# Tokens on ScalarE's queue, and the first quarter of a projection in halves, in a two-layer trunk step

## The chip, the cores and the metric

The kernel runs on one core of a Trainium2 chip. The metric is the device time of one execution in microseconds (us). A core has five engines that run in order, each with its own instruction stream: PE (matrix products), DVE (vector), ACT (ScalarE, activations and copies), POOL (GpSimd) and SP (which mostly issues transfers). Transfers between the chip's memory and the on-core memory are issued by SP or ACT on a hardware queue of each, or by POOL on a software queue, and are carried by 16 DMA engines. A transfer's landing is told by a semaphore; whatever needs it waits for that semaphore.

## What is computed

One inference step of a two-layer trunk for 512 sample tokens and 128 prompt tokens (640 together, width 2048, float32). Cut to what matters here:

```python
sh_p, sc_p, gt_p = modulation(c_ctx, ada_w[layer], ada_b[layer])   # silu(cond) @ w + b, in three parts of 2048
sh_s, sc_s, gt_s = modulation(c, ada_w[layer], ada_b[layer])
hp = rms_norm(xp, norm_g[layer]) * (1.0 + sc_p) + sh_p
hs = rms_norm(xs, norm_g[layer]) * (1.0 + sc_s) + sh_s
...                                                                # mixer: (h @ w_in) -> attention, convolution, gates
xp = xp + gt_p * out_p                                             # out = y @ w_out
xs = xs + gt_s * out_s
```

The first input projection needs h, and h needs the tokens' norms, the scale sc and the shift sh of the first layer. The conditioning matrix `ada_w` is 2048 x 6144 for each layer; it is cut into 12 blocks of 512 columns (4 MB each). Blocks 0 to 3 are the shift, 4 to 7 the scale, 8 to 11 the gate. The change touches the loads and the conditioning ahead of and inside the first input projection.

## The kernel before, in words

*Start.* Small vectors (the two conditions, norms, biases) are loaded into rows (`rows_a`, `rows_b`, L92 to L102), one on SP's queue and ten on ACT's. ACT takes a tanh of the conditions (L109), PE transposes the rows (L113, L114). Then `x_load` issues the tokens on SP's queue: five blocks of 128 tokens, each in two loads of 128 x 1024 (512 KB), into buffers that later hold h. `x_block` transposes a block with PE into PSUM in four groups (L839), copies the groups out (three on DVE, one on ACT, L840), squares and sums on ACT (L844), and has POOL take the power -0.5 (L848). `x_rows` (L854, L855) spreads the norms over a table of rows.

*Conditioning.* `ada_on_pe(l, cb, h, n)` computes n x 128 columns of block cb: it loads 2 MB at a time into one of two buffers (`ada_t`, L154), multiplies with the conditions (L157, 128x512 or, for a half block, 128x256), copies (L160), transposes (L163), reduces and adds the bias on DVE (L165, L145, L134). A whole block is two loads, half a block one. Blocks 4 and 0 give scale and shift for the first quarter of the width; before the change both are computed whole ahead of the projection.

*The projection.* `run_tiles` takes the 2048-wide sum in four quarters of four 128-row pieces each. For six leading tiles it goes quarter by quarter, so that only the part of h that is ready is needed: for each quarter (a unit) it loads the weights (`load_raw`, L233, 256 KB a tile in a whole unit), splits each into a rounded part and a remainder (`split_w`: ACT L220, DVE L221), makes h (`h0_maker`: DVE L878, ACT L882, DVE L883), and multiplies three times per piece and half of the tokens (L255, L256, L257): 144 products for a whole unit of six tiles. Four of the six tiles (`trans`) add the units up in memory: ACT copies the first unit's sums (L319), DVE adds the later ones (L321). Ahead of the second tile of a unit, `ahead` (`ada_group`) computes the two conditioning blocks for the next unit. The last quarter is cut into two halves (`cut`), which have half blocks and loads of 128 KB. The last call of `ada_group` also loads gains, the band and the sink (L71, L863).

*What sets the order.* The program is written in source order, but a scheduler places each engine's instructions and the transfers of each queue by its own costs; the built order of a queue can differ from the source's. Weight buffers (`raw`) are four; the rows at the start use three of them. Transfers from SP and ACT share eight semaphores in turn, so that a transfer also waits until the one that had its semaphore before has landed.

Of the kernel before, what the change touches and what calls it, by code (L numbers as in the profile page):

```python
# [11 lines left out]
F32 = mybir.dt.float32  # L12
# [8 lines left out]
P = 128  # L21
# [20 lines left out]
W_BUFS = 4  # L42
# [11 lines left out]
def trunk_kernel(ctx: ExitStack, tc: tile.TileContext, I: dict, O: dict):  # L54
    nc = tc.nc
# [3 lines left out]
    hpool = ctx.enter_context(tc.tile_pool(name="h", bufs=1))  # L59
# [7 lines left out]
    def psT():  # L67
        return pT.tile([P, 512], F32, tag="T", name="T")
# [14 lines left out]
    ident = const.tile([P, P], F32, name="ident")  # L83
# [5 lines left out]
    open_pool("start")  # L89
    sp = pre = pools["cur"]  # L90
    rows_a = wpool.tile([P, P], F32, tag="raw", name="rows_a")
    nc.sync.dma_start(rows_a[0:16, :], I["c"].rearrange("b (k p) -> (b k) p", p=P))  # L92
    nc.scalar.dma_start(rows_a[16:32, :], I["c_ctx"].rearrange("(k p) -> k p", p=P))
    nc.scalar.dma_start(ident, I["k_ident"])
    nc.scalar.dma_start(rows_a[32:64, :], I["norm_g"].rearrange("l (k p) -> (l k) p", p=P))
    nc.scalar.dma_start(rows_a[64:112, :], I["ada_b"][0].rearrange("(k p) -> k p", p=P))
    rows_b = wpool.tile([P, P], F32, tag="raw", name="rows_b")
    nc.scalar.dma_start(rows_b[0:48, :], I["ada_b"][1].rearrange("(k p) -> k p", p=P))
    nc.scalar.dma_start(rows_b[48:72, :], I["b_conv"][0].rearrange("t (k p) -> (t k) p", p=P))
    nc.scalar.dma_start(rows_b[72:74, :], I["c_out_norm"].rearrange("b (k p) -> (b k) p", p=P))  # L100
    for i, n in enumerate(("a_q_norm", "c_q_norm", "d_q_norm")):
        nc.scalar.dma_start(rows_b[74 + i:75 + i, :], I[n])  # L102
# [15 lines left out]
    norm_g = [vec[:, 0:16], vec[:, 16:32]]  # L118
    ada_b = [vec[:, 32:80], vec[:, 80:128]]
# [23 lines left out]
    def add_bias(l, cb, red, h=0, n=4):  # L143
        fs = slice(cb * 4 + 2 * h, cb * 4 + 2 * h + n)
        V.tensor_tensor(mod[l][:, fs, :], red, ada_b[l][:, fs][:, :, None].to_broadcast([P, n, 2]), op=ALU.add)  # L145

    def ada_on_pe(l, cb, h=0, n=4):

        acc, m, wd = psT(), 32 // n, n * P
        for kt in range(KT):  # L150
            if kt % m == 0:
                w = ada_t[0].rearrange("p (k n) -> p k n", k=m)
                ada_t.reverse()
                nc.sync.dma_start(w, I["ada_w"][l, kt * P:(kt + m) * P, cb * 512 + h * 256:cb * 512 + h * 256 + wd]  # L154
                                  .rearrange("(k p) n -> p k n", p=P))
            g = kt % 4
            PE.matmul(acc[32 * g:32 * g + 32, 0:wd], sT[:, kt, :], w[:, kt % m, :],  # L157
                      start=(kt < 4), stop=(kt >= KT - 4), tile_position=(0, 32 * g))
        sb = ada_sb
        A.copy(sb[:, 0:wd], acc[:, 0:wd])  # L160
        tr = psT()
        for j in range(n):
            PE.transpose(tr[:, j * P:(j + 1) * P], sb[:, j * P:(j + 1) * P], ident)  # L163
# [67 lines left out]
    def load_raw(w_ap, col, qd, js=(0, 4)):  # L231
        raw = wpool.tile([P, js[1] - js[0], P], F32, tag="raw", name="raw")
        nc.sync.dma_start(raw, w_ap[(qd * 4 + js[0]) * P:(qd * 4 + js[1]) * P, col:col + P]  # L233
                          .rearrange("(k p) n -> p k n", p=P))
        return raw
# [3 lines left out]
    def split_w(raw):  # L239
        wh = wpool.tile(raw.shape, F32R, tag="wh", name="wh")  # L240
        wl = wpool.tile(raw.shape, F32R, tag="wl", name="wl")
        split(wh, wl, raw)
        mark[0] = wl[:, 0, 0:1]
        return wh, wl
# [41 lines left out]
            credit[0] -= 1.0  # L286

    def run_tiles(jobs, w_ap, make_h, fill=None, rate=0.0, ahead=None, order=(0, 1, 2, 3), before=None,
                  last=None, by_half=False, trans=[], grace=0, cut=None, summed=None, led=None, fill_from=0):
        if trans:  # L290
            lp = tc.tile_pool(name="lead", bufs=1, side="right")
            lead_pool = lp.__enter__()
# [3 lines left out]
            leads = [n for m in range(len(held) + 1) for n in trans[m:m + 1] + held[m:m + 1]]  # L296
            leads += trans[len(held) + 1:]
        else:
            leads, held, lp = list(range(min(3, len(jobs)))), [], None
        lead = len(leads)  # L300
        pps = {n: (sums[n][:, 0:HALF], sums[n][:, HALF:NT]) if n in trans
               else new_pp(1 + held.index(n) if trans else n) for n in leads}
        units = [(pos, qd, js) for pos, qd in enumerate(order) for js in (cut if cut and pos == 3 else [(0, 4)])]
        for ui, (pos, qd, js) in enumerate(units):
            parts = {n: split_w(load_raw(w_ap, jobs[n][0], qd, js)) for n in leads[:W_BUFS]}
            for hv in [HV[:1], HV[1:]] if by_half and pos == 0 else [HV]:
                for k in range(4 * qd + js[0], 4 * qd + js[1]):
                    make_h(k, hv) if by_half else make_h(k)
                for n in leads:
                    if ahead and n == leads[1] and ui + 1 < len(units):  # L310
                        ahead(*units[ui + 1][1:])
                    if n not in parts:
                        parts[n] = split_w(load_raw(w_ap, jobs[n][0], qd, js))
                    if n in trans:
                        pp = new_pp(0)
                        proj_q(pp, parts[n], qd, pos, alone=True, js=js)
                        for i, sl in HV:
                            if ui == 0:
                                A.copy(pps[n][i], pp[i][:, 0:HALF])  # L319
                            else:  # L320
                                V.tensor_add(pps[n][i], pps[n][i], pp[i][:, 0:HALF])  # L321
# [9 lines left out]
        raws, parts = {}, {}  # L331
# [36 lines left out]
        t = 0  # L368
        if before:
            settle()  # L370
        else:
            n = pending.pop(0)
            begin(jobs[n][1], pps[n])
        for i in range(lead, len(jobs)):
# [3 lines left out]
            for qd in range(4):  # L378
# [5 lines left out]
                if pending and not prep:  # L384
                    n = pending.pop(0)
# [436 lines left out]

    rows = tables[:, 0:NT]

    def x_load(b):
        src = I["x_sample"][0, b * P:(b + 1) * P, :] if b < 4 else I["x_prompt"][0]
        ts = []
        for g in range(2):
            ts.append(hpool.tile([P, 1024], F32, tag=f"h{15 - 2 * b - g}", name="xb"))
            nc.sync.dma_start(ts[g], src[:, g * 1024:(g + 1) * 1024])  # L830
        return ts

    def x_block(b, ts):
        s4 = small.tile([P, 2], F32, tag="s4", name="s4")
        for g in range(4):
            ta = psT()
            for j in range(4):
                o = g % 2 * 512 + j * P
                PE.transpose(ta[:, j * P:(j + 1) * P], ts[g // 2][:, o:o + P], ident)  # L839
            (A.copy if g == 3 else V.tensor_copy)(xT[g][:, :, b * P:(b + 1) * P],  # L840
                                                  ta.rearrange("p (j t) -> p j t", j=4))
            if g % 2 == 0:
                junk = pS.tile([P, 1024], F32, tag="S", name="sqj")
                A.activation(junk, ts[g // 2], AF.Square, accum_out=s4[:, g // 2:g // 2 + 1])  # L844
# [12 lines left out]
    def ada_group(g, js):  # L857
        for cb in (4 + g, g):
            ada_on_pe(0, cb, js[0] // 2, js[1] - js[0])
        if g == 3 and js[1] == 4:  # L860
# [2 lines left out]
            nc.sync.dma_start(band, I["k_band"])  # L863
# [129 lines left out]
    jobs = []  # L993
# [5 lines left out]
    for i in range(4):  # L999
        kv, h = i // 2, 2 * i  # L1000
# [8 lines left out]
    for i in range(4, 8):  # L1009
# [349 lines left out]
    jobs = []  # L1359
# [14 lines left out]
    for n in range(4):  # L1374
        kv, h = n // 2, 2 * n
# [109 lines left out]
```

## Time and profile before

| | us |
|---|---|
| median of three runs | 2332.34 (2330.66 to 2336.76) |
| the profiled execution, device time | 2336.12 |
| its span, first to last instruction | 2334.1 |
| PE busy | 2288.0 (98%) |
| DVE busy | 1566.7 (67%) |
| ACT busy | 928.8 (40%) |

Mean granted clock of PE is 0.995. Times in rows are microseconds from the span's start unless marked ns; a row of the timeline gives start, duration, engine, line, operation, output<-input and the count of merged instructions, and in brackets how long the engine had stood idle before and what it waited for. "SPq" and "ACTq" are the transfer issues of these engines. PEld is PE's weight load, which overlaps PE. A busy PE includes matmuls that overlap each other in its pipeline. The stretch that the change touches is the first 160 us, up to the end of the six leading tiles.

### The profile page before, as it was taken

What the parts mean: (1) busy time and instruction counts of PE and PEld (TensorE: products, weight loads), DVE (VectorE), ACT (ScalarE), POOL (GpSimd) and SP (SyncE); (2) the same over time, 40 slices, a digit from 0 to 9 for tenths busy, and PEclk for the clock granted to TensorE, in tenths of its full rate; (3) what the DMA queues carried; (4) which work ended last, traced back from release to release, by engine and by line L of the source; (5) the groups of instructions that cost most, each with busy time, mean ns of one, the idle gap of its engine ahead of it and who ended that gap; (6) DMA issues with size and microseconds to landing.
All of it is one profiled execution on the core that took longest, in us unless ns stands there. A gap on an engine that the chain in (4) does not pass through costs nothing.

```text
span 2334.1 us, 41243 instructions
## 1 busy us (share of the span) xinstructions
PE 2288.0 (98%) x15924; PEld 2207.8 (95%) x15924; DVE 1566.7 (67%) x3177; ACT 928.8 (40%) x1927; POOL 130.6 (6%) x175
## 2 busy tenths in 40 slices
PE   6999999999999999999999999999999999999999
PEld 3788999999999999999999999999999999999999
DVE  4458886786876663988855755855856754567576
ACT  4325442433422222544554443444344444444343
POOL 0001000000000000000010100101000001000101
PEclk9999999999999999999999999999999999999999
DMA  9984535435355443854431422413423312128542
GB/s 327 330 268 140 158 116 170 141 114 172 115 179 165 151 137 115 273 146 130 150 104 52 136 82 71 140 55 94 124 72 92 107 46 82 46 74 270 181 120 69
DMA packets 386257, 321.92 MB, mean 138 GB/s; under 512 B 18081, under 2 KB 327902, under 8 KB 385550
## 3 DMA queue, kind: packets, MB, share of 16 engines
q1 hardware_dynamic: 378496, 290.96, 40.8%
q0 software_dynamic: 7024, 28.12, 3.3%
q8 instruction: 125, 2.05, 0.4%
q14 instruction: 70, 0.57, 0.1%
q10 hardware_dynamic: 542, 0.22, 0.0%
HBM read 290.79 MB, written 28.44 MB: 137 GB/s over the span
## 4 chain that ended last, share of the span: by engine, by line
PE 89%; DMA 4%; DVE 3%; ACT 2%; issue 1%; SPq 1%; POOL 0%; ACTq 0%; DVEq 0%; POOLq 0%
PE pa L255 10%; PE pb L255 10%; PE pb L256 10%; PE pb L257 10%; PE pa L256 10%; PE pa L257 10%; PE pq L502 4%; PE pq L504 4%; PE pq L503 4%; PE T L680 2%; PE S L692 1%; DMA yin<-yd 1%; PE S L694 1%; PE S L693 1%; PE T L157 1%
## 5 line engine op out<-in xcount | busy, mean ns | idle before, releaser
L220 ACT ACTIVATE wh<-raw 128x512 fp32r<-128x512 f32 (+1 forms) x484 | 302.3, 626 | 798.4 <-PE pb L256 653.7
L221 DVE TENSOR_TENSOR wl<-raw,wh 128x512 fp32r<-128x512 f32 (+1 forms) x484 | 330.4, 683 | 351.2 <-ACT wh L220 324.5
L255 PE MATMUL pa<-h,wh 128*128 128x320 f32 x1760 | 560.9, 319 | 4.4 <-ACT h L220 3.1
L256 PE MATMUL pa<-h,wh 128*128 128x320 f32 x1760 | 547.3, 312 | 1.1 <-DVE h L221 1.1
L257 PE MATMUL pa<-h,wl 128*128 128x320 f32 x1760 | 546.0, 310 | 0.0
L257 PE MATMUL pb<-h,wl 128*128 128x320 f32 x1760 | 545.5, 310 | 0.0
L255 PE MATMUL pb<-h,wh 128*128 128x320 f32 x1760 | 545.4, 310 | 0.0
L256 PE MATMUL pb<-h,wh 128*128 128x320 f32 x1760 | 544.9, 310 | 0.0
L192 DVE SCALAR_TENSOR_TENSOR acc<-adaw,sT,acc 128x512 f32<-128x512 f32 (+1 forms) x600 | 357.9, 639 | 17.5 <-DMA adaw<-in_ada_w 16.8
L255 PEld LDWEIGHTS pa<-h,wh 128*128 128x128 f32 x1760 | 332.1, 189 | 23.9 <-issue 15.1
L256 PEld LDWEIGHTS pa<-h,wh 128*128 128x128 f32 x1760 | 332.6, 189 | 6.3 <-issue 4.2
L257 PEld LDWEIGHTS pb<-h,wl 128*128 128x128 f32 x1760 | 330.9, 188 | 2.9 <-issue 2.9
L257 PEld LDWEIGHTS pa<-h,wl 128*128 128x128 f32 x1760 | 332.0, 189 | 1.2 <-issue 1.2
L255 PEld LDWEIGHTS pb<-h,wh 128*128 128x128 f32 x1760 | 331.0, 188 | 0.9 <-ACT h L882 0.4
L256 PEld LDWEIGHTS pb<-h,wh 128*128 128x128 f32 x1760 | 331.0, 188 | 0.1
L666 ACT ACTIVATE p<-S,nm,rq 128x768 f32<-128x768 f32 (+3 forms) x120 | 101.3, 844 | 116.1 <-DVE nm L661 81.9
L502 PE MATMUL pq<-h,wh 128*128 128x320 f32 x352 | 110.0, 313 | 0.4 <-DVE xr L1068 0.4
L503 PE MATMUL pq<-h,wh 128*128 128x320 f32 x352 | 108.8, 309 | 0.0
L504 PE MATMUL pq<-h,wl 128*128 128x320 f32 x352 | 108.4, 309 | 0.0
L659 DVE TENSOR_REDUCE nm<-S 128x1 f32<-128x768 f32 (+3 forms) x120 | 91.9, 766 | 15.9 <-PE S L694 14.8
L220 ACT ACTIVATE pth<-T 128x512 fp32r<-128x512 f32 (+1 forms) x132 | 66.0, 534 | 71.5 <-PE T L680 71.4
L503 PE MATMUL pq<-T,wh 128*128 128x320 f32 x264 | 81.5, 309 | 0.0
(295 smaller groups left out, 3372.6 us busy)
## 6 DMA issues: line engine op xcount, KB each, us to landing
raw<-in_od_w_in SPq DMA_DIRECT2D x208, 256.0 KB, 2.8
raw<-in_ev_w_in SPq DMA_DIRECT2D x202, 256.0 KB, 3.0
adaw<-in_ada_w SPq DMA_DIRECT2D x192, 256.0 KB, 2.9
ada<-in_ada_w SPq DMA_DIRECT2D x16, 2048.0 KB, 9.4
adaw<-in_ada_w SPq DMA_DIRECT2D x128, 128.0 KB, 2.3
yd<-y POOLq DMA_DIRECT2D x34, 320.0 KB, 2.9
yin<-yd SPq DMA_DIRECT2D x32, 320.0 KB, 4.8
w<-yd SPq DMA_DIRECT2D x32, 320.0 KB, 4.3
```

The source lines that it names most:

```text
L192: V.scalar_tensor_tensor(out=a, in0=w, scalar=sT[:, kt, c:c + 1], in1=a, op0=ALU.mult, op1=ALU.add)
L220: A.activation(hi, x, AF.Copy)
L221: V.tensor_sub(lo, x, hi)
L255: PE.matmul(ps, wh[:, i, :], hi[:, sl], start=(j == js[0] if alone else (pos == 0 and j == 0)), stop=False)
L256: PE.matmul(ps, wh[:, i, :], lo[:, sl], start=False, stop=False)
L257: PE.matmul(ps, wl[:, i, :], hi[:, sl], start=False, stop=(j == js[1] - 1 if alone else (pos == 3 and j == 3)))
L502: PE.matmul(ps, wh[:, j, :], hi, start=(h == 0 and j == 0), stop=False)
L503: PE.matmul(ps, wh[:, j, :], lo, start=False, stop=False)
L504: PE.matmul(ps, wl[:, j, :], hi, start=False, stop=(h == 1 and j == 3))
L659: V.tensor_reduce(nm, s, axis=AX.X, op=ALU.max, negate=True)
L666: A.activation(p[:, 0:n], s, AF.Exp, scale=rsc, bias=nm, accum_out=l)
L680: PE.transpose(t[:, i * P:(i + 1) * P], p, ident)
```

## The change

- The token loads move from SP's queue to ACT's and are written ahead of everything else on ACT. The small loads of `rows_a` move from ACT's queue to SP's, those of `rows_b` to POOL's.
- Ahead of the projection only the first half of blocks 4 and 0 is computed (one 2 MB load each instead of two). The half of block 4 is written between the fourth and the fifth token block; that of block 0 is passed to `run_tiles` as `lead_in`, which calls it behind the loads of the first weights and ahead of their splits.
- The first quarter, like the last, is cut into halves (`pos in (0, 3)`), so the leading tiles go through six units instead of five, and the second halves of blocks 4 and 0 become the `ahead` work of the first unit.
- `keep`, which stores the transposed tokens, counts units and is adapted.

```diff
+    def x_load(b):
+        src = I["x_sample"][0, b * P:(b + 1) * P, :] if b < 4 else I["x_prompt"][0]
+        ts = []
+        for g in range(2):
+            ts.append(hpool.tile([P, 1024], F32, tag=f"h{15 - 2 * b - g}", name="xb"))
+            nc.scalar.dma_start(ts[g], src[:, g * 1024:(g + 1) * 1024])
+        return ts
     nc.sync.dma_start(rows_a[0:16, :], I["c"].rearrange("b (k p) -> (b k) p", p=P))
-    nc.scalar.dma_start(rows_a[16:32, :], I["c_ctx"].rearrange("(k p) -> k p", p=P))
-    nc.scalar.dma_start(ident, I["k_ident"])
+    nc.sync.dma_start(rows_a[16:32, :], I["c_ctx"].rearrange("(k p) -> k p", p=P))
+    nc.sync.dma_start(ident, I["k_ident"])
...
+    xs = [x_load(b) for b in range(5)]
-    nc.scalar.dma_start(rows_b[0:48, :], I["ada_b"][1].rearrange("(k p) -> k p", p=P))
+    nc.gpsimd.dma_start(rows_b[0:48, :], I["ada_b"][1].rearrange("(k p) -> k p", p=P))
...
-        units = [(pos, qd, js) for pos, qd in enumerate(order) for js in (cut if cut and pos == 3 else [(0, 4)])]
+        units = [(pos, qd, js) for pos, qd in enumerate(order) for js in (cut if cut and pos in (0, 3) else [(0, 4)])]
         for ui, (pos, qd, js) in enumerate(units):
-            parts = {n: split_w(load_raw(w_ap, jobs[n][0], qd, js)) for n in leads[:W_BUFS]}
+            raws = {n: load_raw(w_ap, jobs[n][0], qd, js) for n in leads[:W_BUFS]}
+            if ui == 0 and lead_in:
+                lead_in()
+            parts = {n: split_w(raws[n]) for n in raws}
...
-            nc.sync.dma_start(ts[g], src[:, g * 1024:(g + 1) * 1024])
...
-    xs = [x_load(b) for b in range(5)]
-    for b in range(5):
+    for b in range(4):
         x_block(b, xs[b])
-    ada_on_pe(0, 4)
+    ada_on_pe(0, 4, 0, 2)
+    x_block(4, xs[4])
     x_rows((0, 1, 2, 3))
     x_rows((4,))
-    ada_on_pe(0, 0)
...
-        g = {(3, 0): 0, (3, 4): 1, (4, 0): 2, (4, 4): 3}.get((ui, n))
+        g = {(4, 0): 0, (4, 4): 1, (5, 0): 2, (5, 4): 3}.get((ui, n))
...
-              summed=keep, led=even_start)
+              summed=keep, led=even_start, lead_in=lambda: ada_on_pe(0, 0, 0, 2))
```

More of the change, by code (lines that the diff above doesn't have):

```diff
@@ L91, in trunk_kernel @@
     rows_a = wpool.tile([P, P], F32, tag="raw", name="rows_a")
-    nc.sync.dma_start(rows_a[0:16, :], I["c"].rearrange("b (k p) -> (b k) p", p=P))
-    nc.scalar.dma_start(rows_a[16:32, :], I["c_ctx"].rearrange("(k p) -> k p", p=P))
-    nc.scalar.dma_start(ident, I["k_ident"])
-    nc.scalar.dma_start(rows_a[32:64, :], I["norm_g"].rearrange("l (k p) -> (l k) p", p=P))
-    nc.scalar.dma_start(rows_a[64:112, :], I["ada_b"][0].rearrange("(k p) -> k p", p=P))
+    def x_load(b):
[5 more added lines that the diff above has]
+        return ts
+    nc.sync.dma_start(rows_a[0:16, :], I["c"].rearrange("b (k p) -> (b k) p", p=P))
+    nc.sync.dma_start(rows_a[16:32, :], I["c_ctx"].rearrange("(k p) -> k p", p=P))
+    nc.sync.dma_start(ident, I["k_ident"])
+    nc.sync.dma_start(rows_a[32:64, :], I["norm_g"].rearrange("l (k p) -> (l k) p", p=P))
+    nc.sync.dma_start(rows_a[64:112, :], I["ada_b"][0].rearrange("(k p) -> k p", p=P))
+    xs = [x_load(b) for b in range(5)]
     rows_b = wpool.tile([P, P], F32, tag="raw", name="rows_b")
-    nc.scalar.dma_start(rows_b[0:48, :], I["ada_b"][1].rearrange("(k p) -> k p", p=P))
-    nc.scalar.dma_start(rows_b[48:72, :], I["b_conv"][0].rearrange("t (k p) -> (t k) p", p=P))
-    nc.scalar.dma_start(rows_b[72:74, :], I["c_out_norm"].rearrange("b (k p) -> (b k) p", p=P))
+    nc.gpsimd.dma_start(rows_b[0:48, :], I["ada_b"][1].rearrange("(k p) -> k p", p=P))
+    nc.gpsimd.dma_start(rows_b[48:72, :], I["b_conv"][0].rearrange("t (k p) -> (t k) p", p=P))
+    nc.gpsimd.dma_start(rows_b[72:74, :], I["c_out_norm"].rearrange("b (k p) -> (b k) p", p=P))
     for i, n in enumerate(("a_q_norm", "c_q_norm", "d_q_norm")):
-        nc.scalar.dma_start(rows_b[74 + i:75 + i, :], I[n])
+        nc.gpsimd.dma_start(rows_b[74 + i:75 + i, :], I[n])
     ada_t = [pre.tile([P, 4096], F32, name=f"ada{i}") for i in range(2)]
@@ L288, in run_tiles @@
     def run_tiles(jobs, w_ap, make_h, fill=None, rate=0.0, ahead=None, order=(0, 1, 2, 3), before=None,
-                  last=None, by_half=False, trans=[], grace=0, cut=None, summed=None, led=None, fill_from=0):
+                  last=None, by_half=False, trans=[], grace=0, cut=None, summed=None, led=None, fill_from=0, lead_in=None):
         if trans:
@@ L823, in trunk_kernel @@
     rows = tables[:, 0:NT]
[L825 to L831, printed above, removed]
     def x_block(b, ts):
```

## The prediction

> **What bounds the kernel now.** I read the page first, then five stretches of the span, then the issue order of SP's queue, and last the chain of waits up to the first product.
>
> ```profile
> span 2334.1 us, 41243 instructions
> 0.00:49.59 49.59, 27.15 (x165) 13.96 (x165) 18.19 (x46) 20.78 (x37) 3.00 (x9) 0.93 0.95 333
> 49.59:83.00 33.41, 33.41 (x209) 24.32 (x210) 13.81 (x32) 11.42 (x25) 0.00 (x0) 0.95 0.89 315
> 83.00:160.00 77.00, 77.00 (x602) 64.61 (x601) 42.95 (x104) 22.58 (x48) 1.65 (x3) 1.00 0.85 285
> 160.00:250.00 90.00, 86.78 (x616) 82.47 (x614) 75.04 (x162) 44.06 (x104) 7.09 (x8) 1.00 0.56 170
> 250.00:2334.10 2084.10, 2063.66 (x14341) 2022.40 (x14339) 1416.69 (x2836) 829.91 (x1715) 118.83 (x157) 1.00 0.41 124
> ```
>
> In a row of the stretches the first number after the times is PE's busy time; the last two are the DMA share and GB/s. PE is busy 27.2 of the first 49.6 us and without a gap from there to 160. So whatever the change does to PE before the first projection product, and to PE's work after it, comes out at the end one for one. The first stretch is bound by DMA (share 0.95):
>
> ```profile
> 1.20 9.09 SPq L830 DMA_DIRECT2D xb<-in_x_sample  x8
> 11.96 23.93 SPq L154 DMA_DIRECT2D ada<-in_ada_w  x4
> 35.94 5.55 SPq L233 DMA_DIRECT2D raw<-in_ev_w_in  x4
> 12.43 19.82 DMA ada<-in_ada_w
> 43.59 3.33 PE L157 MATMUL T<-ada,sT 128*32 128x512 f32 x16 [3.26 <-DMA ada<-in_ada_w]
> 44.20 2.86 ACT L220 ACTIVATE wh<-raw 128x512 fp32r<-128x512 f32 x4 [5.68 <-DMA raw<-in_ev_w_in]
> 49.59 0.66 PE pa L255 x2
> ```
>
> Tokens (5.2 MB), then 8.4 MB of conditioning, then weights go out on one queue. The weights, issued from 35.94, become usable at 44.20, just after the conditioning load ahead of them (43.59): a queue delivers in its order. The first product stands at 49.59.
>
> **The change, part by part.** The source says: tokens beside the conditioning, two half conditioning blocks instead of two whole ones ahead of the first product, first weights between them. What counts is the order in which the built changed kernel's instructions stand on each queue. SP's, ACT's and DVE's (vector engine), with the semaphores that each waits for (what stands in brackets behind a colon, and in round ones, is my note):
>
> ```
> SP  6 ada0<-in_ada_w 128x16x256
> SP  7 ada1<-in_ada_w 128x16x256
> SP 10 raw_399<-in_ev_w_in 128x2x128 [waits DMAHW3]
> SP 11 gain_rows<-in_d_k_norm [waits DMAHW4: ada1 landed]
> SP 13 sink<-in_a_sink [waits DMAHW6]
> SP 14 raw_401<-in_ev_w_in [waits DMAHW7: ninth token load landed]
> ACT 9 xb<-in_x_prompt (ninth token load) [waits DMAHW7: ada0 landed]
> ACT 12 th<-rows_a   13 sqj   14 wh<-raw_399   15 sqj   16 sqj   17 wh<-raw_401
> DVE wl<-raw_399, xT0, ssx, nsink<-sink, ssx, xT1, xT2, wl<-raw_401
> ```
>
> So the weights are still issued behind both conditioning loads; the gain, band and sink loads, which had stood late, come in between; and a wait for ada1 stands ahead of raw_401. ACT and DVE are in order too: the split of raw_399 stands on ACT behind the first token square, and on DVE ahead of the first copy of transposed tokens. Nearly the whole token stage (squares, copies, transposes) therefore waits for ada1, where before it ran under the conditioning loads.
>
> **When ada1 lands (T1).** Ahead of it go ten token loads of 0.524 MB, two halves of 2.097 MB and 0.2 MB of small loads: 9.6 MB.
>
> ```profile
> 0.00:3.00 3.00, 0.00 (x0) 0.00 (x0) 0.59 (x3) 0.00 (x0) 0.20 (x4) 1.00 0.24 45
> 18.00:21.00 3.00, 2.62 (x19) 1.73 (x17) 2.41 (x6) 2.97 (x7) 0.55 (x1) 1.00 1.03 410
> 126.00:129.00 3.00, 3.00 (x22) 2.97 (x23) 1.40 (x4) 2.10 (x5) 0.00 (x0) 1.00 1.03 329
> ```
>
> Almost nothing moves before 3 us. Then tokens go at some 0.41 MB/us (18 to 21) and half blocks, whose rows are 1 KB, at 0.33 upwards (126 to 129). With 5.4 MB at 0.41 and 4.2 MB at 0.35, T1 = 3 + 13 + 12 = 28. Bounds: all at 0.41 gives 26.4, all at 0.33 gives 32. ACT's queue moves the tokens' issue, not the bytes.
> The Trainium skill's page "DMA: Bandwidth & Descriptors", section "Issuing engines are not separate DMA queues", speaks against the change here: loads started from several engines interleave on the same 16 DMA engines, and only issue time is saved. Its section "Specifications" gives about 358 GB/s from HBM to one core; the 410 above does not agree, so the trace's rate is taken. By 358 alone T1 would be near 30, an estimate, and the end 2 us later.
>
> **From T1 to the first product.**
>
> ```profile
> 133.40 0.43 SPq L71 DMA_DIRECT2D gain_rows<-in_d_k_norm  x1
> 133.88 0.49 SPq L863 DMA_DIRECT2D band<-in_k_band  x1
> 134.41 0.53 SPq L71 DMA_DIRECT2D sink<-in_a_sink  x1
> 135.04 0.38 SPq L233 DMA_DIRECT2D raw<-in_ev_w_in  x1
> adaw<-in_ada_w SPq DMA_DIRECT2D x128, 128.0 KB, 2.3
> L220 ACT ACTIVATE wh<-raw 128x256 fp32r<-128x256 f32 x5 | 2.1, 420 | 11.7 <-PE pb L256 8.6 <-PE Sp L256 3.1
> 10.08 1.03 ACT L844 ACTIVATE sqj<-xb 128x1024 f32<-128x1024 f32 x1
> 11.26 1.03 ACT L844 ACTIVATE sqj<-xb 128x1024 f32<-128x1024 f32 x1
> 26.98 0.59 ACT L840 COPY xT<-T 128x512 f32<-128x512 f32 x1 [2.35 <-PE T L839]
> 36.68 1.28 PE L854 MATMUL T<-ident,rx 128*128 128x128 f32 x10
> 37.77 0.75 ACT L855 COPY tables<-T 128x512 f32<-128x512 f32 x2 [1.66 <-PE T L854]
> 46.43 0.64 ACT wh L220
> 47.05 0.59 ACT L160 COPY ada_sb<-T 128x512 f32<-128x512 f32 x1
> ```
>
> SP issues gain, band and sink (0.43 + 0.49 + 0.53), then raw_401, which lands 2.3 after its issue as other 128 KB loads do: T1 + 4.0 with gaps. Its split (0.42) ends at T1 + 4.4. Then ACT, in order, has seven squares at a pitch of 1.18 (10.08 to 11.26), four copies of 0.59 and two splits of 0.42 to the fourth block's last copy: 11.5, T1 + 15.9. The half block's copy and the fifth token block, whose groups pass through two PSUM tiles in turn, take 4.0 more; the row products and tables 1.2; PE's second half block 1.9, of which 1.5 lies beside the tables' copies; from its copy to the first product 2.5 (47.05 to 49.59): in all 8.1. First product F = T1 + 24 = 52, against 49.6: +2.4. For F - T1 I allow 22 to 26.
>
> **Work left for later.** The second halves of both blocks now come behind the first product.
>
> ```profile
> 124.07 1.86 PE T L157 x32
> 126.72 0.22 PE T L163 x2
> 74.67 1.92 PE L157 MATMUL T<-ada,sT 128*32 128x512 f32 x16
> ada<-in_ada_w SPq DMA_DIRECT2D x2, 2048.0 KB, 7.8
> 82.79 0.31 PE L255 MATMUL pb<-h,wh 128*128 128x320 f32 x1
> 82.93 0.31 PE L256 MATMUL pb<-h,wh 128*128 128x320 f32 x1
> 52.65 0.53 PE pa L256 x2
> L321 DVE TENSOR_TENSOR sum<-sum,pb 128x320 f32<-128x320 f32 x8 | 3.9, 486 | 5.4 <-PE pb L257 5.3
> ```
>
> Each is 1.86 + 0.22 on PE: +4.2 that stood in idle time before.
>
> **A new wait.** One product takes 0.147 (82.79 to 82.93, and so on), a 2 MB load 7.8 when alone, 5.4 behind another (2.1 MB at 0.39, between the rates above), a conditioning piece 1.9 on PE; some 15 products after the idle start take 0.265 each (52.65), 2 us more; there are two buffers. The third load waits for the first half's products: issued at T1 + 15, usable at T1 + 23, in time. The fourth lands at T1 + 30, in time. The next two whole blocks want four loads, each issued when PE has finished with its buffer; by the built order PE is through them after 84, 99, 120 and 120 products. PE finishes the first of them at F + 21 (84 products 12.3, three pieces 5.7, transposes and the slow start 3), so the third load is issued then and lands at F + 28.8, just when wanted (120 products 17.6, four pieces 7.6, the rest 3.6); the fourth follows 5.4 later, at F + 34.2, and is wanted at F + 30.7. Wait 3.5. Bounds 0 (lands together with its predecessor) and 5.4.
>
> **Costed at nothing.** The cut quarter adds six weight issues (0.38 each, 2.3 in all, if SP were not waiting anyway) and eight sums of 0.486 on DVE, which is busy 13.8 of 33.4 us in that stretch; were it full they would cost about 4. The small row loads on POOL are needed by PE only behind the tanh, which waits for ada0. Token loads ahead of the tanh on ACT delay it to ada0's landing, well before T1. From the second quarter on all queues hold the same order as before.
>
> Sum: 2.4 + 4.2 + 3.5 = +10.1. The profiled execution took 2336.1 for its span of 2334.1 and would take 2346; it stands 3.8 above the median of the runs, 2332.3, which is what I forecast from: 2342. About 0.3%, 7 us, is what a measurement here can tell from no change.
>
> **Rivals.**
> - *SP's queue is served first.* No row shows two full queues sharing the DMA engines. If the halves land by 16.5 (3 + 4.2 MB at 0.33), tokens fill up behind them, the ninth at 25.5, and raw_401 lands at 28.2 instead of 32. F = 48.2, sum +6: 2338, or 2336 if the wait is half as long. For it: SP issues ada0 within its first issues. Against: two ACT token loads are out before it.
> - *Half blocks stay slow.* At 0.33 throughout T1 = 32, F = 56, and with a wait of 5: +15.6, 2348. For it: the 329 row; against: 410 for tokens.
> - *The token stage is not held, so the kernel is faster.* One mechanism: weights landing with the tokens, as the source reads, so that ACT and DVE pass their splits without stopping. Tokens are done at 27.6 as before, all 10.4 MB have landed at 30, and from the last weights to the first product it is 3.2 as before (46.43 to 49.59): F = 33, sum -16.6 + 4.2 + 4 = -8.4, 2324. It decides once F is under 42 (49.6 less 4.2 and 3.5), measurably under 35. Against it stand the wait for ada1 ahead of raw_401, and that 9.6 MB can't land by T1 = 11, which F = 35 needs.
> - *Made up later.* PE's idle 3.2 us from 160 to 250 could take up that much: +7, 2339; that stretch moves with PE, so I give it little.
>
> **How the numbers follow.** Forecast 0.55 (own range 2338 to 2347), SP first 0.21, slow halves 0.12, not held 0.07, made up later 0.05. The predicted time is the forecast's, 2342. The range reaches down to SP served first with the short wait and run scatter (2333) and up to slow halves (2349); it leaves out the faster case and the tails. Faster by over 0.3%: 0.07. Within: SP first 0.17, half of made up later, and the forecast's lower edge 0.1, together 0.29. Slower: 0.64.
>
> **What would show it.** Right: ada1 lands at 26 to 32; ACT idles for long ahead of its first two weight splits, waiting for raw; DVE's first token copy comes after that; first product at 50 to 56; 2 half pieces behind it; a PE wait for ada shortly before the second quarter; from 160 on all rows shifted by one constant. Wrong if token copies run before 20, or the first product stands before 45, or the queue order does not hold.

## The result, and the profile after

| | before | after |
|---|---|---|
| median of four runs each, us | 2333.06 (2330.66 to 2336.76) | 2348.28 (2344.88 to 2350.89) |
| profiled execution, us | 2336.12 | 2347.07 |
| its span, us | 2334.1 | 2344.7 |
| first projection product starts at, us | 49.59 | 56.50 |

The changed kernel is slower: ratio 1.0063, 95% interval 1.0043 to 1.0083, or +15.2 us between the medians. The forecast was +10.1.

The spans of the two profiled executions differ by only 10.6. The view of the tile of row tables shows where that comes from. Its columns are the shortest, median and longest instruction in ns, then the start of the first and of the last in us. The first row is the kernel before, the second the one after:

```profile
L603 DVE TENSOR_TENSOR qm<-qx,tables x24: 681/686/693, 195.7 to 2055.6; 128x512 f32<-128x512 f32 x24
```
```profile
L616 DVE TENSOR_TENSOR qm<-qx,tables x24: 680/686/694, 210.0 to 2067.0; 128x512 f32<-128x512 f32 x24
```

At 196 us everything is late by 14.3, at 2056 by 11.4. Nearly all instructions of the two traces stand apart by 14.2 to 14.3 from 178 to 870, and the lead of the kernel before then shrinks in steps. The first one (2.1) lies between 870 and 970, where PE's granted clock dips in the trace of the kernel before (0.83 from 930 to 940) and not in that of the changed one (1.00 from 944 to 954). The programs hold the same work there, and one execution's span scatters that much by itself (the medians' ranges are 6 us wide). So the start of the first of these 24 instructions is used below as the measure of what the first 160 us cost; it is called the shift, and the one above is +14.3. Between the medians stand 15.2.

The timeline of the changed kernel (start, duration, engine, line, operation, output<-input, count; in brackets the idle time ahead and what ended it; SPq and ACTq are issues of transfers):

```profile
0.75 8.59 ACTq L97 DMA_DIRECT2D xb<-in_x_sample  x8
3.41 5.23 SPq L164 DMA_DIRECT2D ada<-in_ada_w  x2
21.52 0.82 ACTq L97 DMA_DIRECT2D xb<-in_x_prompt  x2
22.37 1.28 ACT L119 ACT_TABLE_LOAD   x1 [22.37 <-DMA ada<-in_ada_w]
...
29.89 0.33 SPq L71 DMA_DIRECT2D gain_rows<-in_d_k_norm  x1
30.58 0.42 ACT L230 ACTIVATE wh<-raw 128x256 fp32r<-128x256 f32 x1 [5.57 <-DMA raw<-in_ev_w_in]
31.03 0.42 DVE L231 TENSOR_TENSOR wl<-raw,wh 128x256 fp32r<-128x256 f32 x1 [5.45 <-ACT wh L230]
31.29 11.40 SPq L243 DMA_DIRECT2D raw<-in_ev_w_in  x7
33.81 0.42 ACT L230 ACTIVATE wh<-raw 128x256 fp32r<-128x256 f32 x1 [0.60 <-DMA raw<-in_ev_w_in]
...
44.75 0.58 ACT L845 COPY xT<-T 128x512 f32<-128x512 f32 x1
44.90 1.93 PE L167 MATMUL T<-ada,sT 128*32 128x256 f32 x32 [0.19 <-DVE xT L845]
46.90 7.83 SPq L164 DMA_DIRECT2D ada<-in_ada_w  x2
50.38 0.58 ACT L845 COPY xT<-T 128x512 f32<-128x512 f32 x1 [3.10 <-PE T L844]
51.73 0.75 ACT L860 COPY tables<-T 128x512 f32<-128x512 f32 x2 [0.77 <-PE T L859]
52.36 1.93 PE L167 MATMUL T<-ada,sT 128*32 128x256 f32 x32 [0.45 <-ACT tables L860]
54.42 0.37 ACT L170 COPY ada_sb<-T 128x256 f32<-128x256 f32 x1 [1.94 <-PE T L167]
56.50 0.41 PE L265 MATMUL pa<-h,wh 128*128 128x320 f32 x1 [0.24 <-ACT h L886]
...
90.03 3.36 PE L167 MATMUL T<-ada,sT 128*32 128x512 f32 x16 [4.05 <-DMA ada<-in_ada_w]
```

Read from the top: ACT issues eight token loads by 9.3, and then stands until 21.5 ahead of the ninth, until the first half load of conditioning has landed; the tanh behind it waits too. SP, which waits for the second half load, is free at 29.89. Only then does the first weight split on ACT run (30.58), DVE's split behind it (31.03), and behind that the first copy of transposed tokens. The next two conditioning loads go out at 46.90, and the product at 56.50 comes from a chain of PE, ACT and DVE steps, not from DMA. In the windows of the changed kernel (start and end, length, then PE, PEld, DVE, ACT and POOL busy with counts; then granted clock, DMA share, GB/s) the DMA engines are full up to 27 and nearly idle from 36 to 45, and full again while PE waits ahead of 90:

```profile
3.00:6.00 3.00, 0.00 (x0) 0.00 (x0) 0.00 (x0) 0.00 (x0) 1.46 (x3) 1.00 0.91 318
6.00:9.00 3.00, 0.00 (x0) 0.00 (x0) 0.00 (x0) 0.00 (x0) 0.00 (x0) 1.00 1.02 323
15.00:18.00 3.00, 0.00 (x0) 0.00 (x0) 0.00 (x0) 0.00 (x0) 0.00 (x0) 1.00 1.05 414
...
27.00:30.00 3.00, 0.00 (x0) 0.00 (x0) 0.00 (x0) 0.00 (x0) 0.00 (x0) 1.00 0.73 268
36.00:39.00 3.00, 2.90 (x15) 1.97 (x13) 2.06 (x5) 2.67 (x7) 0.56 (x1) 1.00 0.15 44
42.00:45.00 3.00, 2.50 (x20) 1.77 (x24) 2.61 (x8) 2.90 (x6) 0.55 (x1) 1.00 0.15 44
...
85.00:90.00 5.00, 0.98 (x12) 0.07 (x4) 0.00 (x0) 0.00 (x0) 0.00 (x0) 0.96 1.07 373
```

### The profile page after: what moved, and what is told of

Its sections match the earlier page's. It is cut to its first block, busy times and chain, and to the rows that moved or that the text cites. A ratio compares the mean times of both kernels' runs of the same rounds, so it can differ in the third digit from the quotient of the medians.

```text
span 2344.7 us, 41429 instructions
## 1 busy us (share of the span) xinstructions
PE 2285.0 (97%) x15988; PEld 2207.7 (94%) x15988; DVE 1571.3 (67%) x3196; ACT 929.0 (40%) x1935; POOL 133.0 (6%) x181
## 4 chain that ended last, share of the span: by engine, by line
PE 52%; DVE 2%; DMA 1%; ACT 1%; issue 1%; POOL 0%; SPq 0%; POOLq 0%; DVEq 0%; ACTq 0%
PE pa L265 5%; PE pb L266 5%; PE pb L265 5%; PE pb L267 5%; PE pa L266 5%; PE pa L267 5%; PE pq L515 4%; PE pq L517 4%; PE pq L516 4%; PE T L693 1%; PE S L705 1%; PE S L707 1%; PE S L706 1%; PE T L544 1%; DMA yin<-yd 1%; PE T L754 1%
## 5 line engine op out<-in xcount | busy, mean ns | idle before, releaser
L672 DVE TENSOR_REDUCE nm<-S 128x1 f32<-128x768 f32 (+3 forms) x120 | 91.9, 766 | 15.9 <-PE S L707 14.8
```

The lines of the kernel that those rows point to most:

```text
L672: V.tensor_reduce(nm, s, axis=AX.X, op=ALU.max, negate=True)
```

## The experiments

Two things had to be told apart: whether the held token stage is what makes the kernel slower, or the sharing of the DMA engines by two queues; and what halving the first quarter is worth by itself. All ratios are to the kernel before, with 95% intervals; "first product" is the start of the first projection product.

| kernel | median, us | ratio | first product | shift |
|---|---|---|---|---|
| before | 2333.06 to 2338.14 | | 49.59 | 0 |
| after | 2348.28 | 1.0063 (1.0043 to 1.0083) | 56.50 | +14.3 |
| splits behind the token stage | 2342.89 | 1.0033 (1.0021 to 1.0044) | 48.54 | +6.2 |
| queue move alone | 2351.46 | 1.0068 (1.0056 to 1.0080) | 70.66 | +20.1 |
| halves alone | 2338.54 | 1.0013 (1.0004 to 1.0021) | 40.93 | +0.7 |
| splits behind, prompt loads late | 2339.74 | 1.0015 (1.0006 to 1.0023) | 45.69 | +1.9 |
| halves alone, 1 MB loads | 2335.13 | 0.9999 (0.9987 to 1.0010) | 38.41 | -1.2 |
| halves alone, tokens first | 2337.09 | 1.0007 (0.9998 to 1.0015) | 41.40 | +1.0 |
| halves alone, both of these | 2338.54 | 1.0006 (0.9996 to 1.0016) | 39.16 | 0.0 |
| queue move for the sample, mended | 2341.32 | 1.0024 (1.0015 to 1.0033) | 44.62 | +5.2 |
| before, 1 MB loads | 2333.65 | 0.9982 (0.9973 to 0.9991) | 48.31 | -1.1 |

The first row gives the medians of the kernel before beside the different runs: they differ by some us, so ratios and shifts are compared, not medians. A shift is read from one execution of each kernel. The difference of the medians from the kernel before lies within 2.4 us of it, except for the queue move alone (15.6 against 20.1) and the kernel before with 1 MB loads (-4.5 against -1.1), so shifts that are only a us or two apart are not told apart.

**The first weights' splits behind the token stage.** The changed kernel, with the first unit's splits (and the sign change of the sinks) queued on ACT and DVE behind the last copies of tokens; the loads stay where they are.

```diff
+            if ui == 0 and lead_in:
+                with tc.issue_after(done_x[True]), tc.issue_after(done_x[False]):   # last token copies of ACT, DVE
+                    parts = {n: split_w(raws[n]) for n in raws}
...
+            with tc.issue_after(done_x[False]):
+                V.tensor_scalar(nsink, sink, -1.0, None, ALU.mult)
```

> The changed kernel with one thing moved: the splits of the first unit's weights (on ACT and DVE) and the sign change of the sink are queued behind the last copy of the token stage. Loads, queues and work stay. Theory H (ACT and DVE, in order, are held at those splits until the second half conditioning load has landed at 30): the first token copy on DVE comes at 25 to 26 instead of 31.4, the fourth block's last copy on ACT at 37 to 39 instead of 44.8, the first product at 49 to 50 instead of 56.5; time about 7 us under the changed kernel, 2340 to 2342 beside 2333 for before. Rival W (the loss is the work and waits that the halves leave for later, about 8 us, and the start is bound by the loads anyway): no gain of more than 2 us over the changed kernel, 2346 to 2350. Rival Q (token loads on ACT's queue slow the conditioning loads on SP's): the same as W here.

Measured: first product 48.54, shift +6.2 instead of +14.3, ratio 1.0033. The copies of tokens show what moved; the rows (of the view of tile T) are of before, after and this kernel:

```profile
L840 DVE COPY xT<-T x15: 680/691/692, 12.8 to 26.3; 128x512 f32<-128x512 f32 x15
```
```profile
L845 DVE COPY xT<-T x15: 680/691/692, 31.4 to 49.7; 128x512 f32<-128x512 f32 x15
```
```profile
L849 DVE COPY xT<-T x15: 680/691/692, 24.9 to 41.4; 128x512 f32<-128x512 f32 x15
```

The place of the splits on two in-order engines (with the sign change, which was moved along) costs 8.1 us (14.3 less 6.2). The loads and their queues are those of the changed kernel, so that much is not due to sharing. The stage is still held to 24.9, by the tanh behind ACT's ninth token load.

**The queue move alone.** The kernel before with its token loads on ACT's queue, the rows on SP's and POOL's; nothing is halved.

```diff
+            nc.scalar.dma_start(ts[g], src[:, g * 1024:(g + 1) * 1024])     # x_load, written behind rows_a
-    nc.scalar.dma_start(rows_a[16:32, :], I["c_ctx"].rearrange("(k p) -> k p", p=P))
+    nc.sync.dma_start(rows_a[16:32, :], I["c_ctx"].rearrange("(k p) -> k p", p=P))
...
+        nc.gpsimd.dma_start(rows_b[74 + i:75 + i, :], I[n])
```

> Before with the queue move alone: tokens on ACT's queue, small loads on SP's and POOL's, whole conditioning blocks, uncut first quarter. Theory H: the weights still stand behind two conditioning loads (now 2 MB of a whole block each), token stage held to about 30, the other two conditioning loads issued at 46 to 50, first product at 62 to 68 instead of 49.6 of before; time 2345 to 2352. Rival W: first product and time as before, 2331 to 2336. Rival Q: first product later by the lost rate, 2 to 6 us, time 2335 to 2340.

Measured: ratio 1.0068, shift +20.1, first product at 70.66, later than the 62 to 68 that were expected. The timeline row of its first product, and two windows:

```profile
70.66 0.90 PE L265 MATMUL pa<-h,wh 128*128 128x320 f32 x2 [1.24 <-ACT h L883]
```
```profile
15.00:18.00 3.00, 0.00 (x0) 0.00 (x0) 0.00 (x0) 0.00 (x0) 0.00 (x0) 1.00 1.03 411
42.00:45.00 3.00, 1.90 (x14) 1.49 (x15) 2.41 (x7) 2.14 (x5) 0.55 (x1) 1.00 0.00 0
```

Moving the queues makes the kernel slower without any halving, and by the shift more so than the whole change (the intervals of the two ratios overlap). While both queues are full they move 411 GB/s, no less than the 410 from 18 to 21 of the kernel before, with one; the loss is the DMA time from 36 to 50, which stands nearly unused (0 in the second row) but for 173 GB/s from 39 to 42: token copies run from 22.0 to 46.9, and the next conditioning loads, whose buffers wait for PE's products behind that, go out at 49.66. PE's granted clock reads 0.50 here from 30 to 39 and 1.00 in the changed kernel, but it does not tell the two apart there: the four weight loads of a transpose group take 0.71 us in both up to 37, and 0.42 once the clock is up (from 44.2 here, from 40.6 in the changed kernel). From 60 to 75 the clock here is 0.50 again, around the first product, where the changed kernel has 1.00 from 57 to 85; that may be a part of the 21.1 us and of the 20.1. The median rose by 15.6 against a shift of 20.1; the profiled execution was 17.6 slower. The 2.5 and 4.5 us between come later than 870 us; 2.3 of them are a step between 870 and 970, where the clock of the kernel before dips, and the rest stays open.

**The halves alone.** The changed kernel with the loads back on the queues of the kernel before.

```diff
-            nc.scalar.dma_start(ts[g], src[:, g * 1024:(g + 1) * 1024])
+            nc.sync.dma_start(ts[g], src[:, g * 1024:(g + 1) * 1024])       # x_load, back behind ada_on_pe's definition
-    nc.gpsimd.dma_start(rows_b[0:48, :], I["ada_b"][1].rearrange("(k p) -> k p", p=P))
+    nc.scalar.dma_start(rows_b[0:48, :], I["ada_b"][1].rearrange("(k p) -> k p", p=P))
```

> The changed kernel with the queue move undone: tokens on SP's queue and small loads on ACT's as before; halves, lead-in and cut first quarter stay. In its built order the first weights stand on SP's queue between the two half conditioning loads, and their splits behind the token stage. Theory H: tokens copied from 12 to 27 as before, second half load landed at 29, first product at 33 to 36, then 4.2 us of work left and a wait of about 4 ahead of the second quarter: time 2323 to 2328, faster than before. Rival W: first product early but everything given back and more, 2335 to 2342. Rival Q: 2323 to 2328 as H.

Measured: first product 40.93, earlier by 8.7, and yet a shift of +0.7. The timeline of this kernel, and four windows of it:

```profile
23.54 15.62 SPq L154 DMA_DIRECT2D ada<-in_ada_w  x3
27.38 3.64 PE L157 MATMUL T<-ada,sT 128*32 128x256 f32 x32 [4.67 <-DMA ada<-in_ada_w]
40.93 0.56 PE L255 MATMUL pa<-h,wh 128*128 128x320 f32 x2 [1.22 <-ACT h L885]
...
67.67 0.37 SPq L154 DMA_DIRECT2D ada<-in_ada_w  x1
75.73 3.64 PE L157 MATMUL T<-ada,sT 128*32 128x512 f32 x16 [4.85 <-DMA ada<-in_ada_w]
```
```profile
41.00:50.00 9.00, 9.00 (x81) 7.53 (x85) 4.53 (x12) 3.63 (x11) 0.00 (x0) 1.00 1.08 366
60.00:65.00 5.00, 5.00 (x38) 4.50 (x31) 0.98 (x2) 0.00 (x0) 0.00 (x0) 1.00 0.64 216
65.00:70.00 5.00, 4.24 (x38) 1.74 (x40) 0.84 (x4) 0.58 (x1) 0.00 (x0) 1.00 0.75 247
70.00:75.00 5.00, 0.88 (x11) 0.00 (x0) 1.62 (x4) 0.00 (x0) 0.00 (x0) 0.81 1.05 393
```

The 8.7 are spent again: 4.2 of conditioning products that had stood in idle time, and a wait of 4.85 for the next conditioning load. Together 9.05, and 9.05 less 8.7 is +0.35; the shift is +0.7. The load that PE waits for is issued late, at 67.67, as soon as PE has finished with the buffer that it goes into, and is used at 75.73, 8.1 us later; a 2 MB load alone takes 7.8. The DMA engines have room before that: they move 216 GB/s from 60 to 65 and 247 from 65 to 70, and 393 only in the wait itself. So with two buffers of 2 MB it is the buffers that bind here, not the bytes. The expected gain was wrong in both parts: the first product did not come at 33 to 36, because this order's half loads land late (PE waits 4.67 at 27.38), and what was gained there was taken back. Together with the two runs above: the halves gain 5.8 where the token stage is held (20.1 to 14.3; the clock from 60 to 75 may be a part of that), and nothing where it isn't.

**Splits behind the token stage, and the prompt's loads late.** The first experiment, with the fifth block's two token loads issued on ACT behind the third block's squares and copies, so that the tanh does not stand behind them.

```diff
+    xs = [x_load(b) for b in range(4)]
...
+        if b == 2:
+            with tc.issue_after(done_x[True]):
+                xs.append(x_load(4))
```

> As the run with the splits behind the token stage, and the last two token loads (the prompt) are issued on ACT behind the squares of the third block instead of ahead of the tanh, so that ACT is not held until the first half conditioning load has landed either. Tokens stay on ACT's queue. Theory H: tanh at 9 to 12, the first four token blocks copied by 26; the third conditioning load, part of which PE has ahead of its first product, is issued at about 32 and lands at 40, so first product at 38 to 42; time 2329 to 2335. Rival W: as the changed kernel, 2345 to 2350. Rival Q: no better than the run with the splits behind, 2340 or more.

Measured: first product 45.69, shift +1.9 (from +6.2), ratio 1.0015. The timeline:

```profile
8.29 1.28 ACT L119 ACT_TABLE_LOAD   x1 [8.29 <-DMA rows_a<-in_ada_b]
27.44 0.82 ACTq L97 DMA_DIRECT2D xb<-in_x_prompt  x2
33.85 1.03 ACT L853 ACTIVATE sqj<-xb 128x1024 f32<-128x1024 f32 x1 [4.90 <-DMA xb<-in_x_prompt]
35.31 0.69 PE L173 MATMUL T<-ident,ada_sb 128*128 128x128 f32 x2 [9.12 <-ACT ada_sb L170]
...
78.13 1.92 PE L167 MATMUL T<-ada,sT 128*32 128x512 f32 x16 [3.37 <-DMA ada<-in_ada_w]
```

The tanh's table now loads at 8.29 instead of 22.37, and 4.3 us go. So two holds make up 12.4 of the 14.3: the splits 8.1, the ninth token load 4.3. The first product missed the expected 38 to 42, and the time (2339.74) the expected 2329 to 2335, since the late prompt loads became the new wait: ACT stands 4.90 for them at 33.85, with the copy of the half block's sums behind (PE waits 9.12 for it). The wait of 3.37 ahead of the second quarter stays.

**Halves alone, with conditioning in loads of 1 MB through four buffers.**

```diff
-    ada_t = [pre.tile([P, 4096], F32, name=f"ada{i}") for i in range(2)]
+    ada_t = [pre.tile([P, 2048], F32, name=f"ada{i}") for i in range(4)]
-        acc, m, wd = psT(), 32 // n, n * P
+        acc, m, wd = psT(), 16 // n, n * P
-                ada_t.reverse()
+                ada_t.append(ada_t.pop(0))
```

> The run with the halves alone, and the conditioning loads cut to 1 MB in four buffers instead of 2 MB in two (same memory). Asked: is the 4.85 us wait of PE ahead of the second quarter, which that run shows, one of buffers that come free too late (theory B), or are the loads saturated there (theory L)? By B the wait falls under 2 and the first product comes 1 to 2 earlier (the first MB of the first half is used while the second lands): everything from 160 on 2 to 5 us earlier than with the halves alone, time 2332 to 2336 beside 2338.5. By L the wait stays within 1 of 4.85 and the time within 2.

Measured: first product 38.41, shift -1.2, ratio 0.9999. The waits of PE from 28 to 110, with total, times and longest, and two windows:

```profile
PE T L157 <- DMA ada<-in_ada_w: 1.5, 1, 1.5
```
```profile
38.50:50.00 11.50, 11.50 (x88) 8.05 (x89) 4.27 (x11) 2.60 (x7) 0.00 (x0) 0.85 1.00 329
50.00:60.00 10.00, 10.00 (x73) 7.68 (x73) 5.31 (x14) 5.87 (x16) 0.00 (x0) 1.00 0.76 251
```

The wait falls from 4.85 to 1.5, as expected if buffers come free too late, and not if the loads are saturated. The first product comes 2.5 earlier, but only 1.9 of these 5.9 us arrive. From the first product to the first of the 24 instructions PE has the same 1099 products in both kernels; it is idle 3.5 us less than in the halves alone (4.9 against 8.4) and busy 4.1 us longer (151.2 against 147.1). So the rest goes in slower products: 88 in the first 11.5 us, where the halves alone had 81 in 9. Some 1.7 of the 4.1 (0.15 of 11.5) is the granted clock of 0.85 there, against 1.00 in the halves alone; what the other 2.4 us are stays open.

**Halves alone, with the fifth token block first.** The fifth block and the row products ahead of the first half block, since that waited for its load at 27.38.

```diff
-    ada_on_pe(0, 4, 0, 2)
     x_block(4, xs[4])
...
     x_rows((4,))
+    ada_on_pe(0, 4, 0, 2)
```

> The run with the halves alone, with the fifth token block and the row products written ahead of the first half conditioning block instead of behind it. Theory S (the fifth block, rows and two half blocks stand in series through two PSUM tiles, 13.5 us from the first half's landing to the first product): first product 36 to 38 instead of 40.9. By S with L (loads saturated up to the second quarter) the wait ahead of the second quarter grows by about as much, so that all from 160 on stays within 1.5 and the time at 2337 to 2339; by S with B it comes 3 to 4 us earlier, 2334 to 2336. If S is wrong the first product stays at 40 to 42.

Measured: first product 41.40, shift +1.0, not different from the halves alone (40.93, +0.7). PE waits for conditioning twice up to 110, 8.5 us in all, longest 4.3. The 36 to 38 that were expected if the order of the steps on PE bound the start did not come. The start is bound by the landing of the half loads.

**Both of these.** The halves alone with the 1 MB loads and the fifth block first:

```diff
+    ada_t = [pre.tile([P, 2048], F32, name=f"ada{i}") for i in range(4)]
...
     x_rows((4,))
+    ada_on_pe(0, 4, 0, 2)
```

> Both edits on the halves alone: tokens and rows first, and 1 MB loads in four buffers. By S and B first product at 35 to 37, wait ahead of the second quarter under 2, time 2329 to 2333, below before (2335.9); by L 2336 to 2339.

Measured: first product 39.16, shift 0.0, ratio 1.0006. The expected 35 to 37 and 2329 to 2333 were missed (the median is 2338.54). The two edits do not add up; the shift of the 1 MB loads alone, -1.2, is not improved when tokens come first.

**The queue move, mended.** The changed kernel with all that the runs before spoke for: splits behind the token stage, tokens first, 1 MB loads, and the prompt's two loads on SP ahead of the conditioning, so that ACT issues the four sample blocks alone.

```diff
+            (nc.scalar if b < 4 else nc.sync).dma_start(ts[g], src[:, g * 1024:(g + 1) * 1024])
```

> The changed kernel with its queue move kept for the four sample blocks, the prompt's loads on SP ahead of the conditioning, weight splits queued behind the token stage, tokens and rows ahead of the half blocks, 1 MB loads in four buffers. Asked: does issuing tokens on ACT gain anything once nothing is held behind it? Theory H (only the order of waits was wrong with it) with S and B: first product at 35 to 40, time within 2 of the run with both edits and the tokens on SP, 2329 to 2335. Rival Q (sharing two queues costs the conditioning loads time): first product 3 or more later than in that run, time 2335 or more.

Measured: first product 44.62, shift +5.2, where the run before this one, on SP's queue and without the edit of the splits, has 39.16 and 0.0. Timeline and a window:

```profile
0.75 12.29 ACTq L97 DMA_DIRECT2D xb<-in_x_sample  x8
14.37 0.31 ACT L119 ACTIVATE th<-rows_a 32x128 f32<-32x128 f32 x1
34.07 1.92 SPq L243 DMA_DIRECT2D raw<-in_ev_w_in  x4
36.08 7.57 SPq L164 DMA_DIRECT2D ada<-in_ada_w  x4
43.66 1.03 PE L167 MATMUL T<-ada,sT 128*32 128x256 f32 x2 [5.17 <-DMA ada<-in_ada_w]
```
```profile
33.00:36.00 3.00, 2.51 (x42) 1.27 (x38) 1.81 (x7) 0.57 (x2) 0.00 (x0) 1.00 0.19 54
```

By its numbers this is what the rival of shared queues expected (3 or more later, 2335 or more), and this run alone does not rule out that sharing has a part in it. What the trace shows is a wait that has moved from ACT to SP. The weight loads stand ahead of the conditioning loads on SP, need a buffer whose split is now behind the token stage, and go out at 34.07; DMA is nearly idle meanwhile (54 GB/s), the conditioning goes at 36.08, and PE waits 5.17 for it right ahead of its first product. A better order of all this may exist; none was found in which ACT's queue beats SP's.

**The kernel before, with 1 MB loads.** The same edit of buffers as above, and nothing else:

```diff
+    ada_t = [pre.tile([P, 2048], F32, name=f"ada{i}") for i in range(4)]
+        acc, m, wd = psT(), 16 // n, n * P
+                ada_t.append(ada_t.pop(0))
```

> The kernel before with the conditioning in loads of 1 MB through four buffers, and nothing else. If what the halves lost was bought back by the finer loads alone (theory B: with finer loads PE begins a block's products when half as much has landed), the same edit should gain here too: the first block's products begin earlier, the last piece behind the last load is half as long, first product 47.5 to 49 instead of 49.6, no wait ahead of the second quarter as before, and 2333 to 2335 against some 2336 for the kernel before: within 0.15 per cent. If the finer loads only shorten the wait that the halves brought in, nothing moves: first product at 49.6 and the same time within 0.05 per cent. If 16 more load issues on the queue cost something, the first product comes later than 49.6.

Measured: first product 48.31, shift -1.1, ratio 0.9982 (0.9973 to 0.9991), the only kernel whose whole interval lies below 1, if by less than the 0.3% that the prediction took as what can be told from no change. The shift explains 1.1 of the 4.5 between the medians; the rest comes later or is scatter. The gain at the first product, 1.3, reaches the end here (no wait for conditioning follows), as with halves it did not.

## Why the prediction was right, and where its size was off

- *Direction and mechanism: right.* The splits on ACT and DVE hold the token stage until the second half load has landed: copies start at 31.4 instead of 12.8, and queueing the splits behind them takes 8.1 of 14.3 away. What the source reads like, weights landing with the tokens, did not happen; that rival is refuted by the first weights' split at 30.58. The measured 2348.28 lies just above the forecast's own 2338 to 2347; the whole range holds it because it was stretched to 2349 for the rival of slow halves. The first product, at 56.50, came just behind the 50 to 56 that were named as a sign, and 26.6 behind T1, where 22 to 26 were allowed.
- *T1 = 28: 29.9.* The bytes were right (the ten windows up to 30 add up to 9.86 MB), the rate at the start was not: 318 and 323 GB/s from 3 to 9, and some 360 on average from 3 to 30, where the forecast's terms have 384. Its 0.41 for tokens was read from a window (18 to 21 of the kernel before) in which about half of the bytes were conditioning already. The estimate from the 358 GB/s of the Trainium skill's page "DMA: Bandwidth & Descriptors", section "Specifications", was near 30, and 29.9 was measured, though not because 358 is a limit here: three windows had 400 to 414. What the Trainium skill's same page says in the section "Issuing engines are not separate DMA queues" agrees with the runs: a second queue brought no more bytes (411 GB/s against 410).
- *From T1 to the first product, 24: 26.6.* The second split ended at T1 + 4.3 (4.4 forecast) and the fourth block's last copy at T1 + 15.4 (15.9). The tail was 11.2 instead of 8.1. The first half block's products start at 44.90, with the copies nearly done, and the fifth block's copies follow in turn with it up to 50.96: 5.6 behind the fourth block's last copy, where 4.0 was forecast. PE then waits for ACT's table copy (0.45 at 52.36) before the second half block, of which 1.5 had been placed beside that copy; hardly any of it lay there. These two make up the 3.1.
- *First product +2.4: +6.9.* This is the term that was mis-sized: 1.9 from T1 and 2.6 from the tail.
- *Work left for later, +4.2: 3.8.* From the first product to the first of the 24 instructions PE is busy 3.8 us longer in the changed kernel than before, and idle 3.6 longer (6.6 of 153.5 against 3.0 of 146.1). With the first product these are the whole shift: 6.9 + 3.8 + 3.6 = 14.3. Ten products of the second halves ran ahead of the first product (1.05 at 55.21), which the forecast did not have. The windows, before and after:

```profile
49.59:195.70 146.11, 143.10 (x1031) 120.78 (x1032) 79.73 (x185) 48.89 (x112) 5.03 (x7) 0.99 0.83 280
```
```profile
56.50:210.00 153.50, 146.89 (x1089) 121.25 (x1090) 86.01 (x204) 51.80 (x120) 4.90 (x7) 0.99 0.85 287
```

- *New wait, +3.5: 4.05,* at the place that was named, ahead of the second quarter (90.03), and by the mechanism that was named: the last two loads ahead of it went out at 76.18 and 80.43, when PE had finished with their buffers, and the DMA engines were half idle just before (0.54 from 75 to 80). The halves bring it, not the queues: 4.85 in the halves alone, none in the kernel before. Loads of 1 MB cut it to 1.5.
- *Costed at nothing:* the tanh behind ACT's token loads. It was late as said (22.37), and was not hidden once the splits were out of the way: 4.3. In the changed kernel itself the splits come last, so the sum is not affected.
- *Rivals.* SP's queue first: ada1 landed at 29.9, not 16.5, and the ninth token load was issued at 21.5. Slow half blocks (2348) gave the measured time but for half the reason: T1 29.9 instead of 32, and the rest from the tail. Made up later: the shift was constant from 178 to 870. The next conditioning loads were put at T1 + 15 and went out at T1 + 17.0 (46.90); that the DMA engines would therefore stand nearly idle from 36 to 45 the prediction did not say, though it follows from its own terms.

## What to carry to other kernels

Look up where a load's first consumer stands on its in-order engine, and what the issue of each load waits for: here the place of the first weight splits on ACT and DVE cost 8.1 us and the place of one token load's issue 4.3, while the choice of the queue brought no bytes. Getting the first product earlier is worth little when the work that it leaves behind, and the loads that wait for that work's buffers, come after it: 8.7 us earlier gave nothing in the halves alone, where PE was then 4.0 us longer busy and 5.4 longer idle. To see what a change of the start is worth, compare the start of the same late instruction in both traces rather than single spans, which differed by 4 us for reasons that lie elsewhere.

## What the runs showed of the hardware that was not expected

- A load's issue on ACT waited for an unrelated load on SP's queue: the ninth token load went out at 21.52, with the landing of a 2 MB half load, although its buffer had not been used before. The first eight had gone out by 9.3.
- Two queues together moved 400 to 414 GB/s from 9 to 18 us of the changed kernel, and 318 to 323 in the 6 us before that, when the half loads with rows of 1 KB and the small rows were among them. From 6 to 9 it was the half loads: 0.92 of the 0.97 MB came by SP's queue, and half loads with no tokens beside them moved 327 and 350 GB/s from 48 to 54.
- PE's granted clock at the start differed between kernels that differ little: 0.50 from 30 to 39 in the queue move alone, where PE was busy 1.1, 1.8 and 3.0 of each 3 us, 0.85 from 38.5 to 50 in the halves with 1 MB loads, 1.00 in the halves alone from 41 to 50. A 1.00 at the start of a trace is not always to be trusted: the changed kernel has it up to 37, while the weight loads of its transposes take 0.71 us for four and 0.42 later. The Trainium skill's page "TensorE: Matmul & The Clock Gate", Part 1, has half the clock after an idle window and the full one after some 3.4 us of sustained work; the 0.50 while PE was busy in pieces, and until it had been busy without a gap, agrees with that.
